# Norm factors through scratch memory instead of through TensorE, and a rebuilt last norm, in a conv + SwiGLU layer on one core

## The chip, the core and the metric

The kernel runs on one core of a Trainium2 chip, as one program. A core has TensorE (PE; its weight loads are shown apart as PEld), VectorE (DVE), ScalarE (ACT), GpSimd (POOL) and SyncE (SP, which here only issues DMAs). ACT issues DMAs too. The metric is the time of one execution in microseconds (us).

## The reference

One layer of a hybrid encoder: 2048 tokens (SEQ) of 1024 features (D_MODEL), all float32. The token mixer is a gated convolution of width 3, followed by a SwiGLU network with 2816 inner features. Every sub-layer is normalized before and after, and the result of a projection of a conditioning vector c gives shift, scale and gate.

```python
def rms_norm(x, g):
    xf = x.astype(jnp.float32)
    y = xf * lax.rsqrt(jnp.mean(xf * xf, axis=-1, keepdims=True) + RMS_EPS)
    return (y * g.astype(jnp.float32)).astype(x.dtype)
...
    h = modulate(rms_norm(x, norm_gains[i, 0]), sh_m, sc_m)
    h = short_conv_mixer(h, conv_w_in[j], conv_w[j], conv_w_out[j])
    x = x + g_m[:, None, :] * rms_norm(h, norm_gains[i, 1])
    h = modulate(rms_norm(x, norm_gains[i, 2]), sh_f, sc_f)
    h = swiglu(h, ffn_w_gate_up[i], ffn_w_down[i])
    x = x + g_f[:, None, :] * rms_norm(h, norm_gains[i, 3])
```

So there are four norms, and each needs one factor per token: one over the root of the mean square of that token's 1024 features.

## The kernel before

**Tiling.** Features lie on the 128 partitions, tokens along the free dimension. The 2048 tokens are handled in two units u of 1024, each of two halves tok of 512 (CH). A tile is 128 features by 512 tokens; a half has eight of them (KD). The four products of the layer are phases: `in` (1024 to 3072), `out` (1024 to 1024), `gu` (1024 to 5632) and `down` (2816 to 1024). The order of the phases is in0, out0, in1, out1, gu0, down0, gu1, down1, where the digit is u.

**A product.** Each product is done with seven half-size products P1 to P7 instead of eight (Strassen's scheme in Winograd's form); sums of blocks of weights and of inputs stand ahead of it. Every operand is split into a high part of fewer bits and the rest (`high`, a cast on ACT; `low`, a subtraction on DVE), and each product of two operands takes three matmuls. Results accumulate in PSUM, whose eight banks are handed out by `bank`.

**The order of the work** is written out by hand. `slots` is the list of (phase, group, product); one slot is twelve matmuls of 128x128 by 128x512 for most of them. The loop at the end of the function goes through the slots; at each it supplies weights some slots ahead, runs what is due, and writes that slot's matmuls. `later(n, f)` runs f n slots on, `schedule` at a slot, and a generator started with `run` sleeps n slots at each `yield n`. Every engine works its instructions in the order in which they are written. SP's queue carries all loads and many stores in one order, so a DMA that must wait holds back those behind it; ACT's queue carries some stores between ACT's own instructions. Buffers come from pools of a fixed number (NRAW = 16 `raw` tiles, NRB = 2 `rb` tiles, and so on), and an instruction that takes a buffer waits until its last reader is done.

**A norm factor.** In the phases `out` and `down`, `add_square` squares each finished tile on ACT and adds the squares up on POOL. `norm_of_sums` multiplies the sum with a column of 1/1024 on PE, which gives four columns of 128 tokens in a bank; DVE adds epsilon. `root` raises to the power -1/2 on POOL and refines the result with a step of Newton's on DVE (three operations on 128x4; the factor comes out times -2, which the gains, multiplied by -0.5 at the start, undo). The factor q then has a token on each partition and must be had along the free dimension, the same on every partition: `diagonal` scales the identity with each of q's four columns on DVE, `spread` multiplies a matrix of ones with the result on PE into a bank and copies it to an `rb` tile on ACT, and `spread_later` puts some slots between the two. The tiles of the half are multiplied with it on DVE. The names in the trace are r0 to r3 for the first norm (from rows of x, four quarters of 512 tokens), n, m (spread as h) and o with u and tok for the other three: n00 is the norm after the mixer of unit 0, half 0. A name's last letter says what it is: v the mean square, p the power, t Newton's step, q the factor, d the diagonal, b the spread in PSUM, r the copy.

r2 and r3 come from `norm_of_rows`, which loads 128 whole rows of x at a time and squares them on ACT with a running sum; r0 and r1 are made in `start`.

**The end.** The last half (u = 1, tok = 1) goes through `last_half`, right behind the last product. The tile before the last adds its square to the other six, the last has its own (`lastq`). `last_half` multiplies the two with the column of 1/1024, adds them, makes root, diagonal and spread (`lasts`, `lastv`, `lastp`, `lastt`, `lastd`, `lastb`), and then for each of eight tiles multiplies z with the factor on DVE. For the five tiles of ON_PE the residual x is added on PE (an identity matmul of x laid down earlier, one of z on top, bank `lastx`), copied by ACT and stored from ACT's queue; for the other three DVE adds it and SP stores it. These tiles are `xl` in the trace.

All instructions are recorded under one line, 78, that of the helper which keeps them in order, so they are told apart by the tiles they write and read.

Of the kernel before, what the change touches and what calls it, by code (L numbers as in the profile page):

```python
# [49 lines left out]
def hybrid_conv_layer(  # L50
# [106 lines left out]
    A.activation(cact, vt[:, VC : VC + KD], AF.Silu)  # L157
    V.tensor_scalar(vt[:, VG : VG + 4 * KD], vt[:, VG : VG + 4 * KD], -0.5, None, ALU.mult)
    mA = [const.tile([P, KD], F32, name=f"mA{i}") for i in range(2)]
# [58 lines left out]
    def root(v, name):  # L218

        p, t = small(4, name + "p"), small(4, name + "t")  # L220
        G.tensor_tensor(p, v, mhalf, ALU.pow)
        yield 1
        q = sb.tile([P, 4], F32, tag="q", bufs=8, name=name + "q")
        V.tensor_tensor(t, p, p, ALU.mult)
        V.tensor_tensor(t, t, v, ALU.mult)
        V.scalar_tensor_tensor(q, t, -3.0, p, ALU.add, ALU.mult)
        return q
# [21 lines left out]
    def spread_later(q, name, put, lag=4):  # L249
        dg = diagonal(q, name)  # L250
        yield lag
        put(spread(dg, name))

    def norm_of_sums(acc, name):

        st = bank(name + "s")
        for t in range(4):
            PE.matmul(st[:, t : t + 1], acc[:, t * P : (t + 1) * P], mean, start=True, stop=True)
        v = small(4, name + "v")
        V.tensor_scalar(v, st[:, :4], EPS, None, ALU.add)  # L260
        yield 1
        return (yield from root(v, name))

    def norm_of_rows(g, name, put):
# [4 lines left out]
        def load(k):  # L269
            if k < len(rows):  # L270
                t, i = rows[k]
                xr[k] = raw(f"xr{g}{t}{i}")
                r0 = g * CH + t * P
                SP.dma_start(xr[k], x[r0 : r0 + P, i * CH : (i + 1) * CH])

# [11 lines left out]
        q = yield from root(v, name)  # L287
        yield 1
        yield from spread_later(q, name, put, 6)

# [223 lines left out]
    class Group:  # L514
# [134 lines left out]
        def ready_z(self, c):  # L649
# [7 lines left out]
            if ph.last and ph.tiles_done[1] == KD:  # L657
                ph.sq = tmp("lastq")
                A.activation(ph.sq[:, :CH], z, AF.Square)
                scaled_z()  # L660
            else:
                add_square(ph.acc, tok, z, f"{ph.name}q{tok}{n}", V if ph.last and c == "21" else G, 0.5 if ph.last else 1)
                if ph.last and tok:
                    later(1, scaled_z)
            ph.tile_ready(tok, n, z)
            if ph.tiles_done[tok] == KD:
                ph.half_ready(tok)

    def add_square(acc, key, z, name, E=G, lag=1):
        if key not in acc:  # L670
            acc[key] = tmp(name)
            A.activation(acc[key][:, :CH], z, AF.Square)
        else:
            sq = tmp(name)
            A.activation(sq[:, :CH], z, AF.Square)
            later(lag, lambda: E.tensor_tensor(acc[key][:, :CH], acc[key][:, :CH], sq[:, :CH], ALU.add))
# [259 lines left out]
    def after_out(ph, tok):  # L936
# [4 lines left out]
        q = yield from norm_of_sums(ph.acc[tok], f"n{u}{tok}")  # L941
        yield (24 if u == 0 else 34) + 8 * tok
        yield from spread_later(q, f"n{u}{tok}", partial(put, rb, 0))
        acc = {}
# [21 lines left out]
        yield 7  # L966
        rb1[u, tok] = yield from norm_of_sums(acc[0], f"m{u}{tok}")

    def after_down(ph, tok):
# [7 lines left out]
        q = yield from norm_of_sums(ph.acc[tok], f"o{u}{tok}")  # L977
        if not ph.last:
            yield 22 + 10 * tok
        yield from spread_later(q, f"o{u}{tok}", partial(put, rb, 0), 2 if ph.last else 4)  # L980
        tiles = {}
# [26 lines left out]

    ON_PE = (4, 5, 6, 7, 0)

    def last_half(ph):
# [7 lines left out]

        st = bank("lasts")  # L1020
        for k in ON_PE[:2]:
            add_x(k)
        for i, sq in enumerate((ph.acc[tok], ph.sq)):
            for t in range(4):
                PE.matmul(col(st, 4 * i + t), sq[:, t * P : (t + 1) * P], mean, start=True, stop=True)
        for k in ON_PE[2:]:
            add_x(k)
        v = small(4, "lastv")
        V.tensor_scalar(v, st[:, :4], EPS, None, ALU.add)
        V.tensor_tensor(v, v, st[:, 4:8], ALU.add)  # L1030
        dg = diagonal(at_once(root(v, "last")), "last")
        b = bank("lastb")
        PE.matmul(b, one, dg[:, :CH], start=True, stop=True)
        for k in ON_PE + tuple(k for k in range(KD) if k not in ON_PE):
            z, xt = ph.z(tok, k), ph.xt[k]
            V.tensor_tensor(z, z, b, ALU.mult)
            if k in ON_PE:
                PE.matmul(sums[k], ident, z, start=False, stop=True, skip_group_check=True)
                A.copy(xt, sums[k])
                A.dma_start(out_tile(u, tok, k), xt)  # L1040
            else:
                V.tensor_tensor(xt, xt, z, ALU.add)
                SP.dma_start(out_tile(u, tok, k), xt)
# [314 lines left out]
    for ph in phases[1:]:  # L1358
# [18 lines left out]
        else:  # L1377
            rb = {}
            src = lambda t, tok, kk, u=ph.u: SP.dma_start(t, x1_d[u][tok][:, kk * 4 : kk * 4 + 4, :])
            for tok, op in ((0, "P1"), (1, "P7")):  # L1380
                go = lambda u=ph.u, tok=tok, rb=rb: run(spread_later(rb1[u, tok], f"h{u}{tok}", partial(put, rb, tok)))
                at(op, -14 - 2 * ph.u, go)
            normalized(Features(ph, src, rb, 1), at, 2 * ph.u)
# [100 lines left out]
```

## Time and profile before

| what | value |
|---|---|
| time, median of 3 runs | 1967.44 us (1966.73 to 1967.90) |
| the profiled execution | 1968.11 us |
| its span in the profile | 1966.3 us |
| PE busy | 1939.7 us, 99% |
| DVE busy | 1463.6 us, 74% |
| ACT busy | 870.3 us, 44% |
| POOL busy | 343.1 us, 17% |
| moved by DMA | 459.51 MB, mean 234 GB/s |
| granted clock of PE | 0.999 |

The span is what the profiler saw of the profiled execution, from its first to its last instruction; 1.8 us lie around it. A row of the timeline gives start and length in us, the engine, the operation, and output <- inputs with their shapes; "x8" merges eight of a kind, and what stands in brackets is how long the engine was idle before and which instruction ended that. ACTq and SPq are the DMA issues of those engines. A row of a wait gives the time in all, how often, and the longest. A row of a tile gives the shortest, median and longest duration in ns.

### The profile page before, as it was taken

The numbers are of one execution on the slowest core, as the hardware profiler recorded it, in microseconds if no ns is written. First come the engines' busy times: TensorE is split into PE (matmuls) and PEld (weight loads), VectorE is DVE, ScalarE is ACT, GpSimd is POOL, SyncE is SP. The second block draws the span as 40 slices with busy tenths as digits, with TensorE's granted clock in tenths as the row PEclk, the third lists the DMA queues.
The fourth block names the chain that finished last, engine by engine and source line by source line (L and its number), as shares of the span: only waits on it lengthen the run. The fifth ranks groups of instructions, "written<-read, shape, count | busy, mean of one in ns | idle before, by whom it ended". The sixth has DMA issues, their size and how long they took to land.

```text
span 1966.3 us, 24998 instructions
## 1 busy us (share of the span) xinstructions
PE 1939.7 (99%) x8468; PEld 1572.9 (80%) x8468; DVE 1463.6 (74%) x2159; ACT 870.3 (44%) x1430; POOL 343.1 (17%) x224
## 2 busy tenths in 40 slices
PE   8899999999999999999999999999999999999998
PEld 4578887878888888888888888888888888888886
DVE  5998898978998876997776765586776655665466
ACT  4633457534336643443333454463333333444452
POOL 0012112311221301244331310120100100111010
PEclk9999999999999999999999999999999999999999
DMA  9369979769996764677665987477554342386534
GB/s 389 137 230 378 332 248 352 267 214 362 324 315 236 263 222 148 223 241 248 208 216 186 304 297 261 183 278 267 199 192 135 125 142 97 118 316 229 197 132 133
DMA packets 204752, 459.51 MB, mean 234 GB/s; under 512 B 22864, under 2 KB 38352, under 8 KB 198224
## 3 DMA queue, kind: packets, MB, share of 16 engines
q1 hardware_dynamic: 180000, 403.52, 59.4%
q10 hardware_dynamic: 24624, 54.40, 7.2%
q8 instruction: 66, 1.08, 0.2%
q14 instruction: 62, 0.51, 0.1%
HBM read 326.75 MB, written 131.07 MB: 233 GB/s over the span
## 4 chain that ended last, share of the span: by engine, by line
PE 92%; DVE 3%; issue 2%; DMA 2%; ACT 1%; POOL 0%; ACTq 0%; POOLq 0%; SPq 0%; DVEq 0%
PE gu0P L78 21%; PE gu1P L78 21%; PE in0P L78 11%; PE down0P L78 11%; PE in1P L78 10%; PE down1P L78 9%; PE out1P L78 4%; PE out0P L78 3%; DMA x<-xx 0%; DMA in0a<-xt_d 0%; DMA c<-c_row_d 0%; PE pms L78 0%; DVE down1z L78 0%; DVE in1y L78 0%; DMA in7P2k<-kin7P 0%
## 5 line engine op out<-in xcount | busy, mean ns | idle before, releaser
L78 DVE TENSOR_TENSOR gu1a<-gu1P,gu1a 128x512 f32<-128x512 f32 x63 | 43.5, 691 | 108.7 <-PE gu1P L78 108.7
L78 DVE TENSOR_TENSOR gu0a<-gu0P,gu0a 128x512 f32<-128x512 f32 x63 | 43.3, 688 | 69.5 <-PE gu0P L78 67.7
L78 POOL TENSOR_TENSOR gu1a<-gu1a 128x512 f32<-128x512 f32 x11 | 19.0, 1726 | 363.5 <-DVE gu1g11s L78 42.5
L78 ACT COPY gu1a<-gu1P 128x512 f32<-128x512 f32 x42 | 24.7, 588 | 98.5 <-PE gu1P L78 87.4
L78 POOL TENSOR_TENSOR nq<-nq,nq 128x512 f32<-128x512 f32 x28 | 41.4, 1477 | 133.8 <-ACT nq L78 129.0
L78 ACT COPY gu0a<-gu0P 128x512 f32<-128x512 f32 x42 | 24.5, 588 | 84.3 <-PE gu0P L78 81.5
L78 DVE CUSTOM_DVE_ANT_0 ada<-ada,c 128x512 f32<-128x512 f32 x80 | 60.1, 761 | 0.0
L78 ACT COPY gu1g<-gu1P 128x512 f32<-128x512 f32 x24 | 14.1, 589 | 92.9 <-PE gu1P L78 92.9
L78 POOL TENSOR_TENSOR down0q<-down0q,down0q 128x512 f32<-128x512 f32 x14 | 23.9, 1706 | 144.1 <-ACT down0q L78 144.0
L78 POOL TENSOR_TENSOR gu0a<-gu0a 128x512 f32<-128x512 f32 x11 | 18.2, 1658 | 170.5 <-ACT gu0a L78 47.5
L78 ACT COPY gu0g<-gu0P 128x512 f32<-128x512 f32 x24 | 14.1, 589 | 75.9 <-PE gu0P L78 75.4
L78 POOL TENSOR_TENSOR down1q<-down1q,down1q 128x512 f32<-128x512 f32 x10 | 16.1, 1615 | 148.6 <-ACT down1q L78 148.5
L78 DVE TENSOR_TENSOR gu1g<-gu1P,gu1g 128x512 f32<-128x512 f32 x24 | 16.6, 691 | 27.4 <-ACT gu1g L78 26.0
L78 DVE TENSOR_TENSOR down2P<-down2P,down2P 128x512 fp32r<-128x512 f32 x14 | 12.0, 854 | 28.6 <-ACT down2P L78 28.6
L78 ACT ACTIVATE gu1a<-gu1a 128x512 f32<-128x512 f32 x42 | 26.6, 633 | 13.2 <-DVE xo L78 6.0
L78 ACT ACTIVATE gu0a<-gu0a 128x512 f32<-128x512 f32 x42 | 26.6, 632 | 11.5 <-DVE gu0a L78 10.2
L78 POOL TENSOR_TENSOR out1q<-out1q,out1q 128x512 f32<-128x512 f32 x14 | 22.3, 1594 | 51.3 <-ACT out1q L78 51.2
L78 POOL TENSOR_TENSOR out0q<-out0q,out0q 128x512 f32<-128x512 f32 x14 | 22.5, 1606 | 45.1 <-ACT out0q L78 44.9
L78 DVE TENSOR_TENSOR xx<-xx,zz 128x512 f32<-128x512 f32 x32 | 28.2, 880 | 1.1
L78 DVE TENSOR_TENSOR gu0g<-gu0P,gu0g 128x512 f32<-128x512 f32 x24 | 16.5, 689 | 14.7 <-ACT gu0g L78 13.3
L78 ACT ACTIVATE nq<-xx 128x512 f32<-128x512 f32 x32 | 20.2, 631 | 15.9 <-DVE xx L78 15.9
L78 DVE TENSOR_TENSOR down10P<-down10P,down10P 128x384 fp32r<-128x384 f32 x14 | 8.6, 615 | 22.0 <-ACT down10P L78 22.0
(3225 smaller groups left out, 6728.5 us busy)
## 6 DMA issues: line engine op xcount, KB each, us to landing
ada<-ada_d SPq DMA_DIRECT2D x64, 256.0 KB, 5.2
act0A<-gu0a SPq DMA_DIRECT2D x33, 256.0 KB, 3.5
act1A<-gu1a SPq DMA_DIRECT2D x33, 256.0 KB, 2.7
ada<-ada_d SPq DMA_DIRECT2D x16, 512.0 KB, 9.4
zz<-z SPq DMA_DIRECT2D x32, 256.0 KB, 5.5
xx<-xt_d SPq DMA_DIRECT2D x32, 256.0 KB, 5.4
x<-xx ACTq DMA_DIRECT2D x32, 256.0 KB, 5.5
down0S<-act0S SPq DMA_DIRECT2D x8, 1024.0 KB, 7.1
```

Of the source, the lines that this page charges most:

```text
L78: return tc.keep_in_program_order(f(*args, **kwargs))
```

## The change

Twelve of the factors (r2, r3, n00 to n11, the four of m, o00 and o01) are no longer spread by diagonal, matmul and copy. `keep_row` stores q, as it is, from ACT's queue to 512 floats of scratch memory, and `repeat_later` loads these 512 floats into all 128 partitions of an `rb` tile through SP's queue. For the factor to come out in token order, q must hold token 4p + t in column t of partition p. So the squares of those norms are written in another order (ACT reads a tile along the tokens and writes with a step of 128 elements), and the rows of x for r2 and r3 are read every fourth.

The step of Newton's goes from `root`, in all places, and the factor of -0.5 on the gains with it.

At the end, the sums of the first seven tiles' squares are multiplied out ahead of the last products (`all_but_one`); the diagonal is multiplied with the ones quarter by quarter; two matmuls into a bank that nobody reads (`lastw`) follow; ON_PE has four tiles; two of the additions go to POOL; the order of the tiles is another one.

```diff
-    V.tensor_scalar(vt[:, VG : VG + 4 * KD], vt[:, VG : VG + 4 * KD], -0.5, None, ALU.mult)
...
     def root(v, name):
 
-        p, t = small(4, name + "p"), small(4, name + "t")
-        G.tensor_tensor(p, v, mhalf, ALU.pow)
+        q = sb.tile([P, 4], F32, tag="q", bufs=8, name=name + "q")
+        G.tensor_tensor(q, v, mhalf, ALU.pow)
         yield 1
-        q = sb.tile([P, 4], F32, tag="q", bufs=8, name=name + "q")
-        V.tensor_tensor(t, p, p, ALU.mult)
-        V.tensor_tensor(t, t, v, ALU.mult)
-        V.scalar_tensor_tensor(q, t, -3.0, p, ALU.add, ALU.mult)
         return q
...
+    def keep_row(q, name, lag=8):
+
+        row = scratch([CH], name + "w")
+        later(lag, lambda: A.dma_start(row.rearrange("(p t) -> p t", t=4), q))
+        return row
+
+    def repeat_later(row, name, put, lag=8):
+        rb = sb.tile([P, CH], F32, tag="rb", bufs=NRB, name=name + "r")
+        SP.dma_start(rb, row.rearrange("(a n) -> a n", a=1).to_broadcast((P, CH)))
+        yield lag
+        put(rb)
...
-                r0 = g * CH + t * P
-                SP.dma_start(xr[k], x[r0 : r0 + P, i * CH : (i + 1) * CH])
+                in_turn = x[g * CH : (g + 1) * CH, i * CH : (i + 1) * CH].rearrange("(p t) c -> p t c", t=4)
+                SP.dma_start(xr[k], in_turn[:, t, :])
...
         q = yield from root(v, name)
-        yield 1
-        yield from spread_later(q, name, put, 6)
+        row = keep_row(q, name, 2)
+        yield 7
+        yield from repeat_later(row, name, put, 6)
...
                 if ph.last and tok:
                     later(1, scaled_z)
+                    if ph.tiles_done[1] == KD - 1:
+                        later(1.5, partial(all_but_one, ph))
...
-    def add_square(acc, key, z, name, E=G, lag=1):
+    def add_square(acc, key, z, name, E=G, lag=1, in_turn=True):
+        def square(t):
+            if in_turn:
+                A.activation(t[:, :CH].rearrange("p (t n) -> p n t", t=4), z.rearrange("p (n t) -> p n t", t=4), AF.Square)
+            else:
+                A.activation(t[:, :CH], z, AF.Square)
...
         q = yield from norm_of_sums(ph.acc[tok], f"n{u}{tok}")
-        yield (24 if u == 0 else 34) + 8 * tok
-        yield from spread_later(q, f"n{u}{tok}", partial(put, rb, 0))
+        row = keep_row(q, f"n{u}{tok}")
+        yield (20 if u == 0 else 30) + 8 * tok
+        yield from repeat_later(row, f"n{u}{tok}", partial(put, rb, 0))
...
-        rb1[u, tok] = yield from norm_of_sums(acc[0], f"m{u}{tok}")
+        q = yield from norm_of_sums(acc[0], f"m{u}{tok}")
+        rb1[u, tok] = keep_row(q, f"m{u}{tok}")
...
-        if not ph.last:
-            yield 22 + 10 * tok
-        yield from spread_later(q, f"o{u}{tok}", partial(put, rb, 0), 2 if ph.last else 4)
+        if ph.last:
+            yield from spread_later(q, f"o{u}{tok}", partial(put, rb, 0), 2)
+        else:
+            row = keep_row(q, f"o{u}{tok}")
+            yield 18 + 10 * tok
+            yield from repeat_later(row, f"o{u}{tok}", partial(put, rb, 0))
...
-    ON_PE = (4, 5, 6, 7, 0)
+    ON_PE, ON_POOL, LAST_TURN = (4, 5, 6, 7), (1, 2), (0, 4, 1, 5, 6, 2, 7, 3)
+
+    def sums_of_squares(ph, sq, first):
+        for t in range(4):
+            PE.matmul(col(ph.st, t + 4 * first), sq[:, t * P : (t + 1) * P], mean, start=True, stop=True)
+
+    def all_but_one(ph):
+        ph.st = bank("lasts")
+        sums_of_squares(ph, ph.acc[1], True)
...
-        st = bank("lasts")
+        v = small(4, "lastv")
+        V.tensor_scalar(v, ph.st[:, 4:8], EPS, None, ALU.add)
         for k in ON_PE[:2]:
             add_x(k)
-        for i, sq in enumerate((ph.acc[tok], ph.sq)):
-            for t in range(4):
-                PE.matmul(col(st, 4 * i + t), sq[:, t * P : (t + 1) * P], mean, start=True, stop=True)
+        sums_of_squares(ph, ph.sq, False)
         for k in ON_PE[2:]:
             add_x(k)
-        v = small(4, "lastv")
-        V.tensor_scalar(v, st[:, :4], EPS, None, ALU.add)
-        V.tensor_tensor(v, v, st[:, 4:8], ALU.add)
-        dg = diagonal(at_once(root(v, "last")), "last")
-        b = bank("lastb")
-        PE.matmul(b, one, dg[:, :CH], start=True, stop=True)
-        for k in ON_PE + tuple(k for k in range(KD) if k not in ON_PE):
+        V.tensor_tensor(v, v, ph.st[:, :4], ALU.add)
+        q = at_once(root(v, "last"))
+        dg = tmp("lastd")
+        b, warm = bank("lastb"), bank("lastw")
+        for t in range(4):
+            c = slice(t * P, (t + 1) * P)
+            V.tensor_scalar(dg[:, c], ident, q[:, t : t + 1], None, ALU.mult)
+            PE.matmul(b[:, c], one, dg[:, c], start=True, stop=True)
+        for _ in range(2):
+            PE.matmul(warm, one, dg[:, :CH], start=True, stop=True)
+        for k in LAST_TURN:
...
-                V.tensor_tensor(xt, xt, z, ALU.add)
+                (G if k in ON_POOL else V).tensor_tensor(xt, xt, z, ALU.add)
...
-                go = lambda u=ph.u, tok=tok, rb=rb: run(spread_later(rb1[u, tok], f"h{u}{tok}", partial(put, rb, tok)))
-                at(op, -14 - 2 * ph.u, go)
+                go = lambda u=ph.u, tok=tok, rb=rb: run(repeat_later(rb1[u, tok], f"h{u}{tok}", partial(put, rb, tok)))
+                at(op, -18 - 2 * ph.u, go)
```

More of the change, by code (lines that the diff above doesn't have):

```diff
@@ L661, in ready_z @@
             else:
-                add_square(ph.acc, tok, z, f"{ph.name}q{tok}{n}", V if ph.last and c == "21" else G, 0.5 if ph.last else 1)
+                add_square(ph.acc, tok, z, f"{ph.name}q{tok}{n}", V if ph.last and c == "21" else G, 0.5 if ph.last else 1, not ph.last)
                 if ph.last and tok:
                     later(1, scaled_z)
+                    if ph.tiles_done[1] == KD - 1:
+                        later(1.5, partial(all_but_one, ph))
             ph.tile_ready(tok, n, z)
@@ L667, in ready_z @@
                 ph.half_ready(tok)
-    def add_square(acc, key, z, name, E=G, lag=1):
+    def add_square(acc, key, z, name, E=G, lag=1, in_turn=True):
[4 more added lines that the diff above has]
+                A.activation(t[:, :CH], z, AF.Square)
         if key not in acc:
             acc[key] = tmp(name)
-            A.activation(acc[key][:, :CH], z, AF.Square)
+            square(acc[key])
         else:
             sq = tmp(name)
-            A.activation(sq[:, :CH], z, AF.Square)
+            square(sq)
             later(lag, lambda: E.tensor_tensor(acc[key][:, :CH], acc[key][:, :CH], sq[:, :CH], ALU.add))
```

## The prediction

> **What bounds the kernel now.** I read the page of the profile first, then PE's own waits, then the chain of waits in order of time.
>
> ```profile
> span 1966.3 us, 24998 instructions
> PE 1939.7 (99%) x8468; PEld 1572.9 (80%) x8468; DVE 1463.6 (74%) x2159; ACT 870.3 (44%) x1430; POOL 343.1 (17%) x224
> ```
> ```profile
> 250.00:300.00 50.00, 50.00 (x220) 41.04 (x219) 46.97 (x102) 25.91 (x54) 3.17 (x2) 1.00 0.78 256
> ```
>
> The second fence has a window: from:to, their length, and busy time of PE, weight loads, DVE, ACT and POOL with counts, granted clock, DMA share, GB/s. PE works for all but 26.6 us of the span. So whatever PE does not have to do anywhere between shortens the run, unless another engine sets the pace at that place. PE's waits (time, count, longest) name such places; those that the change can touch are:
>
> ```profile
> PE in1P L78 <- ACT in1c L78: 2.3, 2, 1.4
> ...
> PE out0P L78 <- ACT out0z L78: 1.7, 1, 1.7
> ...
> PE r1b L78 <- DVE r1d L78: 0.6, 1, 0.6
> ...
> PE in1P L78 <- DMA in7P2k<-kin7P: 0.4, 1, 0.4
> ```
>
> All of these fall before 480 us; from there to the tail PE never idles. The spreads of the norm factors are links of the chain (start, length, what):
>
> ```profile
> 266.19 0.86 PE r2b L78 x2
> ...
> 318.88 0.86 PE r3b L78 x2
> ...
> 361.65 16.32 PE in1P L78 x72
> ...
> 442.19 0.86 PE n00b L78 x2
> ...
> 648.14 0.86 PE h00b L78 x2
> ...
> 1435.14 0.86 PE o01b L78 x2
> ```
>
> From r2b to o01b these are twelve (r2b, r3b, n00b, n01b, n10b, n11b, h00b, h01b, h10b, h11b, o00b, o01b), each 0.86 us of PE. That of the last phase's first half stays.
>
> **The change, part by part.**
>
> *Twelve factors through scratch.* Each loses four DVE scalings of the identity, the 0.86 us on PE and an ACT copy; it gains a store on ACT's queue and a load on SP's. The PE term is 12 x 0.86 = 10.3 us. The lower bound counts only the eight after 600 us, where PE never waits: 6.9 us.
>
> What is moved: each load is issued eight slots before its factor is handed on (six for r2 and r3). A slot is twelve matmuls, 2.72 us (72 in 16.32 us at in1's start), so the lead is 16 to 22 us. The broadcast load of the kernel before, a store of ACT's queue (median us to landing last), and a long wait of SP's queue (in down0) say whether that is enough:
>
> ```profile
> L78 SPq DMA_DIRECT2D c<-c_row_d x8: 327/330/491, 206.7 to 1193.1; - x8
> DMA to landing us min/median/max: 3.7/5.6/8.0
> ...
> x<-xx ACTq DMA_DIRECT2D x32, 256.0 KB, 5.5
> ...
> SPq L78 <- ACT down0z L78: 20.4, 4, 16.3
> ```
>
> The same kind of load landed in 8.0 us at most, so I cost it at nothing. The row's store is issued 12 slots (33 us) before the load, five slots (14 us) for r2 and r3, against the same 8 us; the load therefore finds its row written, and SP, whose queue holds every weight load behind it, should not stop. The two rb buffers are no wait either: n00r serves eight tiles in 19 slots, until 442 + 52 = 494 us, and h00's load comes at 648 - 22 = 626. ACT's queue trades a 0.58 us copy for a 0.34 us issue. r2 and r3 come six slots, 16 us, later: 319 + 16 = 335 us for r3, and in1 begins at 361.65.
>
> *DMA traffic.* Twelve broadcasts add 256 KB each. It matters in one place:
>
> ```profile
> 440.00:450.00 10.00, 10.00 (x44) 7.94 (x43) 5.15 (x9) 3.86 (x8) 0.12 (x1) 1.00 1.03 375
> ...
> 470.00:480.00 10.00, 9.60 (x43) 7.63 (x42) 9.86 (x15) 4.25 (x8) 3.05 (x3) 1.00 1.00 359
> ```
>
> In these windows the DMA engines are full. n01's load, 0.26 MB at 359 GB/s, is 0.7 us, and PE's 1.7 us from n00b and n01b may be waited for again: 0 to 2.4 us lost. I take 0.9, since PE waited only 0.4 us there before.
>
> *Newton's step goes from every root.* Three small DVE operations each. Off the path this is nothing, except at two places. At r1, DVE is the late engine (PE waits 0.6 us for r1d):
>
> ```profile
> 50.87 0.16 DVE L78 TENSOR_TENSOR r1t<-r1p 128x4 f32<-128x4 f32 x1
> ...
> 51.34 0.69 DVE L78 TENSOR_TENSOR in0A12l<-in0b,in0A12h 128x512 fp32r<-128x512 f32 x1
> ```
>
> From 50.87 to 51.34 is 0.47 us; I take 0.4 (0 to 0.47). The second place is r3, where PE's 1.71 us stall at 315.86 begins on DVE:
>
> ```profile
> 308.36 1.25 DVE L78 TENSOR_TENSOR r3t<-r3p 128x4 f32<-128x4 f32 x1
> ...
> 311.13 1.90 DVE L78 TENSOR_SCALAR r3d<-ident,r3q 128x128 f32<-128x128 f32 x4
> ...
> 312.95 0.67 DVE L78 TENSOR_TENSOR out0z<-out0P,out0z 128x512 f32<-128x512 f32 x1
> ...
> 313.66 0.63 ACT L78 ACTIVATE out0q<-out0z 128x512 f32<-128x512 f32 x1 [1.87 <-DVE out0z L78]
> ...
> 315.86 0.73 PE L78 MATMUL out0P<-out0S10h,out0P 128*128 128x512 f32 x2 [1.71 <-ACT out0z L78]
> ```
>
> PE waits for an ACT copy that stands behind a square, and the square waits for a DVE addition held up by r3's Newton step and diagonal: 3.4 us that all go. What is late next is the Silu and the weight cast between, so I take 1.4 of the 1.71 (0 to 1.71).
>
> *Squares written in another order.* ACT reads along the row and writes with a step of 128 elements. No row shows a stepped write on ACT; plain squares take 0.632 us (POOL's sums of them 1.3 to 1.7):
>
> ```profile
> L78 ACT ACTIVATE nq<-xx x32: 617/632/637, 462.5 to 885.5; 128x512 f32<-128x512 f32 x32
> L78 POOL TENSOR_TENSOR nq<-nq,nq x28: 1283/1454/1756, 468.9 to 886.2; 128x512 f32<-128x512 f32 x28
> ...
> 330.00:375.00 45.00, 45.00 (x204) 37.38 (x203) 41.59 (x54) 29.59 (x49) 18.49 (x12) 1.00 0.78 275
> ...
> 394.18 1.91 ACT L78 CAST in1S4h<-in1b 128x2048 fp32r<-128x2048 f32 x1 [5.05 <-DVE in1b L78]
> ```
>
> The cast of 2048 elements takes 1.91 us, so an element costs (1.91 - 0.63)/1536 = 0.83 ns and 0.43 us of a square are streaming. The bounds are no change and a doubled stream, 1.06 us. ACT is 29.6 of 45 us busy where out0's squares lie densest; all 16 of that phase would add 16 x 0.43 = 6.9 us, which fits, so I take zero and keep 6.9 as the far end. [...]
>
> *Rows read every fourth* are the same 2 KB pieces: nothing, covered by a load issued two slots (5.4 us) ahead.
>
> *The end.*
>
> ```profile
> 1941.04 0.68 DVE L78 TENSOR_TENSOR down1q<-down1q,down1q 128x512 f32<-128x512 f32 x1
> ...
> 1941.56 0.62 PE L78 MATMUL down1P<-down1A221h,down7P 128*128 128x512 f32 x2
> ...
> 1948.04 0.95 PE L78 MATMUL lasts<-mean,down1q 128*128 128x1 f32 x8
> ...
> 1948.85 1.03 PE L78 MATMUL lasts<-mean,lastq 128*128 128x1 f32 x8
> ...
> 1949.92 0.16 DVE L78 TENSOR_SCALAR lastv<-lasts 128x4 f32<-128x4 f32 x1 [2.70 <-PE lasts L78]
> ...
> 1951.41 0.16 DVE L78 TENSOR_TENSOR lastt<-lastp 128x4 f32<-128x4 f32 x1 [1.13 <-POOL lastp L78]
> ...
> 1952.00 0.87 DVE L78 TENSOR_SCALAR lastd<-ident,lastq 128x128 f32<-128x128 f32 x4
> ...
> 1954.09 3.68 DVE L78 TENSOR_TENSOR down1z<-down1z,lastb 128x512 f32<-128x512 f32 x6 [1.22 <-PE lastb L78]
> ...
> 1960.45 0.69 DVE L78 TENSOR_TENSOR xl<-xl,down1z 128x512 f32<-128x512 f32 x1
> ...
> DMA  0000000000000000049294999999999972000000
> ```
>
> The sums of seven tiles move ahead of the last products. They free 0.8 us of the tail (1948.04 to 1948.85) and cost PE the same 0.8 plus about 0.2, because the accumulator they read is ready at 1941.72 and PE gets there at 1941.56: -0.2. The early epsilon saves its operation of 0.16, Newton 1952.00 - 1951.41 = 0.6. From the diagonal's start to the first multiplication is 2.09 us; in quarters it is 0.87 for the scalings and one quarter's two passes, which I put at 0.5 (bounds: 0.25, two passes as short as those of the sums, and 1.1, as now), so 0.7 is saved (0.1 to 0.9). Together 1.3 us. The turn behind it has one DVE addition less: 8 x 0.61 + 2 x 0.69 = 6.3 us against 7.05 (1954.09 to 1961.14); two additions go to POOL (1.3 to 1.5 us each, beside the multiplications). r3t's 1.25 us against r1t's 0.16 was a DVE operation beside such a POOL addition, so the last DVE addition, due after 5.6 us, may wait for POOL's second one, 4.4 + 1.4 = 5.8: 0.2 us, inside the bounds. But the stores fill the DMA engines: the last row is their busy share in fortieths of 1950 to 1967 us, and from 1957.2 to 1964.0 eight tiles pass, about 0.8 us each. After, the first tile leaves alone; the second, multiplied after 1.9 us, copied as long after that as now (1956.00 for 1954.77), is issued near 3.8 us, and seven tiles follow one another to about 3.8 + 0.6 + 7 x 0.8 = 10.0 us after the first multiplication; before, 1964.0 - 1954.09 = 9.9. So -0.1, and **1.2 us** for the end (0.3 to 2.2).
>
> The sum is 10.3 + 1.4 + 0.4 + 1.2 - 0.9 = 12.4 us. The profiled execution took 1968.11 us, 0.67 above the median of the runs, 1967.44. 1968.11 - 12.4 = 1955.7, and on the scale of the median **1955.0 us**.
>
> **The rivals.**
>
> *The early spreads buy nothing.* DVE is 94% busy from 250 to 300 us, and DMA full from 440 to 490. Then r2b, r3b, n00b, n01b come back as waits (3.4 us) and r3's stall stays: 6.9 + 0.4 + 1.2 = 8.5 us, 1958.9. Against it: PE is busy for 50.00 of those 50 us, with DVE already that full.
>
> *Slow squares.* If each square of out0 delays the ACT copy for which PE waits, 6.9 us are given back: 1961.9. For it: PE's stall at 315.86 is such a copy. Against: out1, with as many squares, has no PE wait at all. [...]
>
> *More stalls dissolve.* The two waits for in1c (2.3 us) and the one for in7P2k are ACT and SP queues running late; if they go and the traffic costs nothing, 12.4 + 0.9 + 2.7 = 16.0 us, 1951.4.
>
> *Slower: SP stops at the new loads.* If a row's store is late, the load waits at the head of SP's queue and the weights behind it. SP's wait of 16.3 us in down0 passed without PE stopping, so this decides only where a store comes more than some 16 us too late; with 1.4 us of PE idle behind each of the twelve, 16.8 us are lost and it comes out near 1971. Against it: the stores of ACT's queue landed in 5.5 us.
>
> *Nothing changes*: the freed PE time reappears as waits everywhere. Without an idle PE after 480 us there is no sign of it.
>
> **How the numbers follow.** Forecast 0.51, early spreads 0.20, more stalls dissolve 0.14, slow squares 0.08, no change 0.04, slower 0.03. The likeliest gives 1955.0. The range from 1951.2 to 1961.0 takes in the first three cases, 0.85, and leaves the squares' far end out. A difference under 0.2%, 3.9 us, cannot be told from none. All of the first four gain more than that: faster 0.93, same 0.04, slower 0.03.
>
> **What would show it.** PE instructions fall by 24 passes for the twelve spreads; the chain has no r2b to o01b, and PE's gaps after 480 us stay at zero. The 1.71 us wait near 313 us is gone or under 0.5; r1's wait is shorter. The squares' row says 0.63 or 1.06. From the last product's end to the first multiplication before is 7.6 us, after about 5.4. Loads of rows land in under 10 us and SP never waits for a row. It is wrong if PE gains waits on ACT in out0, on DMA between 430 and 500 us, or behind an SP wait for a row.

## The result, and the profile after

The changed kernel takes **1964.32 us** in the median (1960.68 to 1966.38, 17 runs), the kernel before 1967.44 (17 runs beside it): ratio 0.9981, 95% interval 0.9974 to 0.9989. The gain is 3.1 us where 12.4 was forecast. That is under the 6.4 us at the lower end of the predicted range, and under the 3.9 us that the prediction held to be indistinguishable from none, although with 17 runs the interval does exclude no change. The profiled execution took 1963.37 us. Its page begins:

```profile
span 1961.6 us, 24893 instructions
PE 1934.4 (99%) x8450; PEld 1569.8 (80%) x8450; DVE 1446.7 (74%) x2061; ACT 898.0 (46%) x1417; POOL 344.9 (18%) x226
```

PE is busy 5.3 us less than before, where the twelve spreads alone were to take off 10.3, so half of that is missing from PE's own work too; the span is 4.7 us shorter. PE's waits of after (time, count, longest):

```profile
PE r0b L78 <- DVE r0d L78: 3.8, 1, 3.8
PE in1P L78 <- ACT in1c L78: 3.4, 2, 2.6
...
PE out0P L78 <- ACT out0z L78: 1.7, 1, 1.7
...
PE gu0P L78 <- ACT gu0a L78: 0.6, 1, 0.6
...
PE in1P L78 <- ACT in1b L78: 0.4, 1, 0.4
...
PE in1P L78 <- ACT in1C L78: 0.3, 1, 0.3
```

The wait for r0d was 0.2 us before; by 127 us nothing of it is left. The wait for in1c has grown from 1.4 to 2.6 us, the one for out0z is as long as before but at another place, and those for gu0a (711 us), in1b and in1C stand behind 480 us, where there were none. Laying PE's instructions of the two traces side by side shows where the change gains and loses. This is the ledger (us, negative is gained; it adds up to the span's difference within 0.4):

| place in the trace of before | after against before |
|---|---|
| head, to 127 us | 0.0 |
| the twelve spreads, together | -10.6 |
| 301.6 | +0.7 |
| the stall at 315.86 / a new one at 321 | -1.9 / +1.8 |
| 433.7, the wait for in1c | +1.1 |
| 435 to 437 | +1.6 |
| 484, 541, 549, 563 | +1.5 |
| 711, the wait for gu0a | +0.8 |
| 895 | +0.2 |
| the end | -0.3 |

The largest loss is the one at 433 to 437 us. The chain of waits of after, from 425 us (start, length, what), and PE's timeline behind it show it:

```profile
425.68 6.79 DMA kgu0P<-gu0P
...
433.06 0.59 ACT in1c L78
```
```profile
433.69 0.73 PE L78 MATMUL in1P<-in1S1h,in0P 128*128 128x512 f32 x2 [2.60 <-ACT in1c L78]
...
435.40 1.06 PE L78 MATMUL in1P<-in1S1h,in0P 128*128 128x512 f32 x2
```
```profile
434.70:438.20 3.50, 3.50 (x10) 2.76 (x9) 1.07 (x2) 0.00 (x0) 3.46 (x2) 0.53 0.90 314
```

The store of kgu0P, 512 KB, lands 6.8 us after its issue. ACT's queue stands still until then, because the buffer that is being stored is to be written again, and the copy in1c, for which PE waits, stands behind it in that queue. The last fence is a window (length, busy of PE, weight loads, DVE, ACT, POOL, granted clock, DMA share, GB/s): behind the wait the clock is granted at 0.53, so PE is "busy" and does 10 matmuls, where the kernel before does 17 in the same 3.50 us at a clock of 1.00. The trace's clock record has it at a half for 3.413 us, from 434.9 us on, which costs 1.7 us. I call this a half-speed window. The record of after has two more ahead of the tail, from 15.1 and 73.1 us, and that of before one, from 83.9 us, each 3.413 us long. One execution of each kernel was profiled, and the granted clock of the 17 runs of the change goes from 0.995 to 0.998, so by my estimate the number of such windows (one takes off 0.0009, half of 3.413 us in 1962) is not the same in each.

Squares with a stepped write, and the end:

```profile
L78 ACT ACTIVATE nq<-xx x32: 1114/1162/1177, 462.8 to 884.5; 128x512 f32<-128x512 f32 x32
```
```profile
1937.39 1.05 PE L78 MATMUL lasts<-mean,down1q 128*128 128x1 f32 x8
...
1943.19 1.88 PE L78 MATMUL lastx<-xl,ident 128*128 128x512 f32 x4
...
1948.77 0.69 DVE L78 TENSOR_TENSOR down1z<-down1z,lastb 128x512 f32<-128x512 f32 x1 [0.66 <-PE lastb L78]
```
```profile
DMA  0000000000000078000099999999999961000000
```

The square went from 0.632 to 1.162 us. The last row is the DMA engines' busy share in fortieths of 1945 to 1962 us: the first tile leaves alone, then comes a hole, then all others at full share. The rows' loads land in under 10 us, as forecast; the slowest:

```profile
L78 SPq DMA_DIRECT2D h01r<-m01w x1: 320/320/320, 639.6 to 639.6; - x1
...
DMA to landing us min/median/max: 8.7/8.7/8.7
```

But SP's queue did stop for DMAs of rows (time, count, longest, between 300 and 330 us):

```profile
SPq L78 <- DMA r3w<-r3q: 4.9, 1, 4.9
...
SPq L78 <- DMA r3r<-r3w: 1.5, 1, 1.5
```

Two more such stops follow, 0.9 us for n01r and 0.8 for h00r, 8.1 us in all. In none does a row's load wait for its store. In the traces the DMAs of SP and ACT signal their landing on eight semaphores, shared out evenly (1421 DMAs before, 177 or 178 on each; 1445 after, 180 or 181), and in all landings recorded no DMA is issued before the last one on its semaphore has landed: SP stopped ahead of a load of `ada` which uses semaphore 108, as r3's store does; that store lands at 319.08 us and the load is issued at 319.14. In both traces there are at most eight DMAs under way, and each row's store and load takes one of these eight places.

### The profile page after: what moved, and what is told of

The parts are those of the page before. It is cut to its first block, busy times and chain, and to the rows that moved or that the text cites. A ratio compares the mean times of both kernels' runs of the same rounds, so it can differ in the third digit from the quotient of the medians.

```text
span 1961.6 us, 24893 instructions
## 1 busy us (share of the span) xinstructions
PE 1934.4 (99%) x8450; PEld 1569.8 (80%) x8450; DVE 1446.7 (74%) x2061; ACT 898.0 (46%) x1417; POOL 344.9 (18%) x226
## 3 DMA queue, kind: packets, MB, share of 16 engines
q8 instruction: 66, 1.08, 0.2%
## 4 chain that ended last, share of the span: by engine, by line
PE 81%; DVE 9%; DMA 5%; ACT 3%; issue 2%; SPq 0%; ACTq 0%; POOL 0%; DVEq 0%
PE gu1P L78 21%; PE gu0P L78 20%; PE down0P L78 11%; PE down1P L78 11%; PE in0P L78 9%; PE in1P L78 4%; PE out1P L78 2%; PE out0P L78 1%; DMA x<-xx 1%; PE pms L78 1%; DMA kgu0P<-gu0P 0%; DVE in1b L78 0%; DMA xr<-x_d 0%; DMA out2P<-w_out_d 0%; DVE in1y L78 0%
## 5 line engine op out<-in xcount | busy, mean ns | idle before, releaser
L78 ACT ACTIVATE nq<-xx 128x512 f32<-128x512 f32 x32 | 37.1, 1159 | 15.7 <-DVE xx L78 15.7
L78 ACT ACTIVATE down0q<-down0z 128x512 f32<-128x512 f32 x16 | 18.5, 1153 | 14.9 <-DVE down0z L78 14.8
```

The costliest lines, as they stand in the source:

```text
L78: return tc.keep_in_program_order(f(*args, **kwargs))
```

## The experiments

Ratios are to the kernel before, run on the same chip beside each; half their intervals is about 0.0009, 1.7 us, so a difference between two of them carries about 2.5 us. "Of after" means an edit of the changed kernel. The diffs are cut at `...`.

**e1_plain_squares**, of after: the squares as before; the order is made where the sums are read.

```diff
-            PE.matmul(st[:, t : t + 1], acc[:, t * P : (t + 1) * P], mean, start=True, stop=True)
+            part = acc[:, :CH].rearrange("p (n t) -> p t n", t=4)[:, t, :] if in_turn else acc[:, t * P : (t + 1) * P]
+            PE.matmul(st[:, t : t + 1], part, mean, start=True, stop=True)
```

> The changed kernel with the squares written in plain order again; the order that the stored factors need comes from the weight loads of the sums, which read every fourth column of the accumulator. The results stay the same. Theory S (the stepped squares, 1.15 us for 0.63, hold up ACT and with it PE in in1, out1 and gu0): the squares fall back to 0.63 us, PE's waits at 541, 564 and 711 us go (2.5 us with what they drag along), and the time is 2 to 3 us under the changed kernel's, about 1961.5. Theory P (the time won early is paid back by loads and DVE chains whatever the squares cost): no change, 1964.3 within 1 us.

Measured: 1967.45, ratio 0.9998 (0.9989 to 1.0007), slower than the change, which neither theory had. The stepped read has a price of its own. The weight loads of one sum, in this run and in after (shortest/median/longest, ns):

```profile
L78 PEld LDWEIGHTS m01s<-mean,nq x8: 308/329/332, 559.6 to 561.2; 128*128 128x128 f32 x8
```
```profile
L78 PEld LDWEIGHTS m01s<-mean,nq x8: 187/192/192, 560.4 to 561.3; 128*128 128x128 f32 x8
```

Each of the ten sums holds PE 1.89 us for 1.04, 8.5 us in all, yet the run lost only 3.1 against the change. The ledger says where part of the rest went: +3.2 us against after at 377 us had become -0.9 by 479. Half of this is one half-speed window of 1.7 us for another: this run has one at 321.7 us and none at 434.9. The rest is 1.7 us of two longer sums, which came back by 400 us; PE's wait of 0.85 us for in1c at 395 us of after is gone, for one. So PE work added there came out nearly even, as PE work removed did. The stall at 321 us stands in this run too (1.8 us), so the stepped squares didn't make it; the one at 711 is gone. The run can't price the squares; e4 does.

**e4_stepped_squares**, of before: only the squares' write is stepped (so the factors fall on other tokens than they should).

```diff
+        def square(t):
+            if in_turn:
+                A.activation(t[:, :CH].rearrange("p (t n) -> p n t", t=4), z.rearrange("p (n t) -> p n t", t=4), AF.Square)
...
-            A.activation(sq[:, :CH], z, AF.Square)
+            square(sq)
```

> The kernel before with nothing but the squares of all norms but the last phase's written with a step of 128 elements; spreads, Newton's step and end as before. The factors then fall on other tokens of the same half; the work is the same. Theory S: ACT's squares take 1.15 us and the time rises by 1 to 3 us to about 1969.5. Theory P: ACT has room, 1967.4 within 0.7 us.

Measured: 1968.57, ratio 1.0001 (0.9992 to 1.0010). A square nearly twice as long costs the kernel before nothing that can be measured.

**e2_spreads_on_pe**, of after: spreads, squares and rows as before; the power alone and the new end stay. **e3_old_end**, of after, with the end of before. **e8_power_only**, of before, without Newton's step and its scaling.

```diff
-        row = keep_row(q, f"n{u}{tok}")
-        yield (20 if u == 0 else 30) + 8 * tok
-        yield from repeat_later(row, f"n{u}{tok}", partial(put, rb, 0))
+        yield (24 if u == 0 else 34) + 8 * tok
+        yield from spread_later(q, f"n{u}{tok}", partial(put, rb, 0))
```

> The changed kernel with the twelve factors spread by diagonal, matmul and copy as before, squares and rows in plain order: what is left of the change is the root without Newton's step and the rebuilt end. If the end and Newton's step are worth what the prediction gave them (1.2 + 1.8 us): 1964.4. If they are worth next to nothing (0.2 us at the end, r3's stall only moved): 1967, and the change's gain of 3.1 us lies in the spreads alone.

> The changed kernel with the end of the kernel before (its root without Newton's step). If the rebuilt end is worth 1.2 us without Newton's 0.6: 1965.0. If the profile's ledger is right (0.2 us in all): 1964.3 to 1964.5, the changed kernel's own time.

> The kernel before with the Newton step alone taken out (with the scaling of vt that served it); nothing else is changed, so this parts the 2.3 to 2.7 us that the run with spreads on TensorE gained into Newton and new end. If Newton's leaving is the gain (the old end in the whole change was no slower, 1963.6): 1965.2, with the stall at 315.86 down from 1.7 to 0.5 us and the wait at 433 at 1.1. If the new end is: 1967.4.

Measured: e2 1965.2, 0.9984 (0.9976 to 0.9993); e3 1963.64, 0.9979 (0.9970 to 0.9988); e8 1965.11, 0.9990 (0.9981 to 0.9998). Newton's leaving is worth about 2 us alone. What the new end is worth is not shown: without it the change is no slower (e3), while e2, which has it, is 0.0006 or 1.2 us ahead of e8, which has not, and both differences lie within 2.5 us of none. All twelve spreads together, beside the power and the end, change the ratio from 0.9984 to 0.9981 only.

**e6_code_shift**, of after: short products in the head, where PE waits for r0d anyway. **e11_before_shifted**, of before: three warm-up products for eight. Both are meant only to move PE's instructions, and with them the loading of PE's code, against the work. The diff is e6's:

```diff
         warm(8)
+        for _ in range(9):
+            PE.matmul(b[:, :16], one, w[:, :16], start=True, stop=True)
```

> The whole change, with nine short products (16 columns, 18 passes, 36 instructions of TensorE) behind the warm-up of the head, where TensorE waits 3.8 us anyway. Theory F (TensorE's code is loaded in blocks of 16 KB, 256 instructions, one block holding one of the 16 DMA engines for 0.93 to 1.25 us; with fewer instructions ahead a block came into the middle of the store of kgu0P at 425.7 us, 3.2 us behind its issue where it had been 0.3 us, and made the wait at in1c 1.2 us longer and the half-speed window behind it): the block comes about 4 us sooner against the work, the store lands 5.4 us after its issue and not 6.8, the wait at 433 falls from 2.6 to about 1.4 us, the window of 434.8 to 438.2 is gone: 1964.3 - 1.2 - 1.6 = 1961.5. Rival R (the rows' own traffic or their DMA issues delay that store): nothing changes there, 1964.3.

> The kernel before with three warm-up products in the head for eight, so that TensorE's code runs 20 instructions later against the work and nothing else changes. Theory F (the position of the code blocks against the store of kgu0P): the block at 427.1 us comes some 2 us behind the store's issue, as in the change, the store lands 6.6 to 6.8 us after its issue for 5.5, the wait at 433 rises from 1.4 to 2.3 to 2.6 us, perhaps with a half-speed window behind it: 1968.5, with the window 1970. If the blocks don't matter: 1967.4 and 1.4 us.

Measured: e6 1961.57, 0.9972 (0.9961 to 0.9982). The median is what theory F said, but against the change the gain is 2.75 us by the medians, 1.8 by the ratios, whose intervals overlap, and 1.4 between the two profiled executions. PE at the same place in e6:

```profile
432.56 0.73 PE L78 MATMUL in1P<-in1S1h,in0P 128*128 128x512 f32 x2 [0.78 <-ACT in1c L78]
```

The wait is 0.8 us for 2.6, and no half-speed window follows it. But in e6 one stands at 321.6 us, behind a wait of 1.8 us, where after had none behind 1.7; this is why the profiled executions differ by half of the forecast only. The busy share of the DMA engines from the issue of that store to its landing, in fortieths, in after (425.7 to 432.5 us) and in e6 (426.4 to 431.4), with the queue that brings code:

```profile
DMA  9999711339999999999998510101000000000959
...
q8 instruction: 1, 0.02, 0.9%
```
```profile
DMA  9999945421635999896999989998886610000000
```

In after the transfer is nearly through at slice 23, 429.6 us, and then single packets trickle (24 GB/s, one packet of 4 KB in each slice of 0.17 us) until near 432. The code block came at 428.99 us and took 0.98, to 429.97; from 429.95 to 432.00 ten packets of 4 KB follow one another end to end. The trace has 16 signals of the store's landing: fifteen by 430.30 us, the last at 432.46, 2.2 us behind (in before by 431.68 and at 432.44, 0.8 behind). In e6 the block had come before the store, and there is hardly such a tail. All profiled kernels at this store:

```
                     block behind the     issue to the cast
                     store's issue, us    that waits for it, us
before, e2, e4, e5, e8, e10, e13, e14
                     -0.1 to 0.5          5.4 to 5.7
e7, e12              0.5, 0.0             5.6, 6.0
e1, after, e3        1.9, 3.3, 3.4        6.6, 6.9, 6.7
e9, e6               -2.2, -2.5           5.3, 5.0
e11                  3.9                  4.8
```

So with a block 1.9 to 3.4 us behind the issue the store is 0.9 to 1.2 us later than in the kernel before; far ahead of it or behind the transfer's bulk the store is sooner. Kernels that load the early rows stand in three of these lines (e7 and e12; e1, after and e3; e6), so it is not the rows that part them. e11 came out at 1969.33 (1.0010, 1.0001 to 1.0018), near the forecast, but not for its reason: the block overshot the store (3.9 us behind the issue, where about 2 was meant), PE's wait there fell to 0.6 us, and the time was lost in the head, 2.3 us by 90 us, where PE had two half-speed windows (13.9 to 20.8 us) behind the shorter warm-up. So only e6 tested the blocks as forecast. In the trace of before there are 66 such blocks (`q8 instruction: 66, 1.08` on its page), 16 KB each, on 17,030 instructions of PE, one per 258, where theory F has 256; that they are PE's code follows from their moving with PE's instructions, 5.8 us sooner against the store with 36 more ahead (e6) and 3.6 later with 20 fewer (e11).

**e7_rows_unused**, of e2: every row is stored and loaded where the change does it, into the buffer that the copy of the product then overwrites. **e12_rows_narrow**: the same with each load to one partition. **e14_places_only**: the same without stores and loads. **e13_stores_only**: e2 with the stores alone. The diff shows e7's way of taking a factor, against the changed kernel:

```diff
         rb = sb.tile([P, CH], F32, tag="rb", bufs=NRB, name=name + "r")
         SP.dma_start(rb, row.rearrange("(a n) -> a n", a=1).to_broadcast((P, CH)))
-        yield lag
-        put(rb)
+        yield lag - 4
+        dg = diagonal(q, name)
+        yield 4
+        put(spread(dg, name, rb))
```

> The run with all spreads on TensorE, Newton step gone and the new end (1965.2), and beside it every row stored and loaded at the same places as in the change, into the same buffer, which the copy of TensorE's product then overwrites: the traffic and the issues of the rows without their saving. Theory R (the rows' stores and loads cost time in the stretches bound by DMA): the waits of the change come back at 433 (2.6 us) and between 479 and 563 (+1.2), with a half-speed window or two: 1967.5 to 1969. Theory F (it is where the code blocks fall, and TensorE's instructions are as many as before): 1965.2, the wait at 433 at 1.1 us.

> The run with all spreads on TensorE and every row stored and loaded unused (1970.1), but each row's load goes to one partition, 2 KB and not 256 KB; the stores, every issue and its place stay, and the copy of TensorE's product overwrites what is loaded. Theory D (the 12 x 256 KB that the loads move are what costs): the waits go, back to the run without rows, 1965.2. Rival I (the issues on SP and ACT, and the stores in 16-byte pieces): 1970.1. Of the 4.9 us between, what remains is the issues' and stores' share.

> The run with all spreads on TensorE (1965.2), and beside it each factor's store to scratch, 12 issues on ACT with 128 pieces of 16 bytes each; no row is loaded, and every spread stands where it stood. Theory S16 (the stores are what the rows cost, through their pieces or the 12 issues of 0.33 us on ACT): 1968 to 1969. Rival Z (the later place of r2 and r3, or the loads' issues): 1965.2.

> The run with every row stored and loaded unused (1970.1; with narrow loads 1969.3), without the stores and without the loads: what stays of it is the place of r2's and r3's products, six slots later, and that the factors' buffers are taken when the loads would be issued. Theory Z (the place): 1968 to 1969. Rivals S16 and the loads' issues: 1965.2. What is left between this run, the stores alone and 1969.3 is the issues of the loads on SP.

Measured, as a ladder: e2 0.9984, e14 0.9985 (1965.35 us; 0.9976 to 0.9994), e13 0.9994 (1967.09; 0.9986 to 1.0003), e12 1.0006 (1969.29; 0.9997 to 1.0015), e7 1.0014 (1970.13; 1.0005 to 1.0023). The places cost nothing that can be measured. Stores and loads together cost 0.0030, 5.9 us, give or take 2.5: some 2 us for the stores, 2.4 for the issues of the loads, 1.6 for their 3 MB. Each of these three steps is no larger than its uncertainty, so the sum is shown and its parts are not: e13 lies between its two theories, e12 near rival I. e7 is above what theory R said, but PE's wait at 433 stayed at 1.3 us, as theory F had it. PE's instructions are as many in e7 as in e2 (17,044 and 17,043), and the code block falls on the store alike. The windows show the cost as idle PE, in e2 and in e7 (columns as above):

```profile
300.00:345.00 45.00, 44.22 (x191) 35.34 (x190) 39.41 (x57) 35.86 (x60) 12.89 (x8) 1.00 0.93 343
430.00:490.00 60.00, 58.87 (x256) 47.95 (x256) 49.01 (x81) 23.69 (x42) 10.59 (x7) 1.00 1.00 355
500.00:700.00 200.00, 200.00 (x892) 164.60 (x891) 185.09 (x282) 106.28 (x181) 45.28 (x30) 1.00 0.81 283
```
```profile
300.00:345.00 45.00, 42.70 (x182) 34.13 (x183) 37.23 (x56) 33.93 (x56) 14.97 (x8) 1.00 0.92 337
430.00:490.00 60.00, 57.42 (x247) 45.86 (x246) 48.70 (x80) 23.09 (x41) 9.54 (x7) 1.00 0.96 336
500.00:700.00 200.00, 198.88 (x888) 163.88 (x887) 184.30 (x280) 103.95 (x179) 46.68 (x31) 1.00 0.82 287
```

In these windows PE is idle 1.9 us in e2 and 6.0 in e7; the change has 6.1 (it is busy for 42.59, 56.93 and 199.39 us). By the ledger of e7 against e2, 3.9 of 4.7 us are lost by 617 us, so it is mostly the early rows that cost. Between 500 and 700 us PE is busy for the whole 200.00 in every kernel without early rows (before, e2, e4, e5, e8, e9, e10, e14) and for 198.66 to 199.68 in every one with them, e13's mere stores included.

**e5_late_rows**, of after: rows only for n10, n11, h10, h11, o00, o01; the other six factors through PE. **e9_longer_warm_up** and **e10_sums_later** are e5 with `warm(12)` for `warm(8)`, and with `later(2.5, ...)` for `later(1.5, ...)` ahead of `all_but_one`.

```diff
-        row = keep_row(q, f"n{u}{tok}")
-        yield (20 if u == 0 else 30) + 8 * tok
-        yield from repeat_later(row, f"n{u}{tok}", partial(put, rb, 0))
+        if u == 0:
+            yield 24 + 8 * tok
+            yield from spread_later(q, f"n{u}{tok}", partial(put, rb, 0))
+        else:
+            row = keep_row(q, f"n{u}{tok}")
...
```

> The change with its rows kept only for the later norms (n10, n11, h10, h11, o00, o01); the factors r2, r3, n00, n01, h00, h01 go through TensorE as before, with plain squares. Theory E (the early rows' savings are paid back before 712 us, the late ones are kept): the gain of the run with all spreads on TensorE (1965.2) stays, and six passes of 0.87 us come off: 1965.2 - 5.2 = 1960.0, with no PE wait over 1.2 us at in1c near 433. Rival K (rows bring a cost wherever they are): the late ones bring no more than the early ones did, 1963.5 to 1964.5.

> The run with the late rows alone (1960.8) and, in the head, twelve warm-up products for eight. That run's trace has two half-speed windows from 13.7 to 20.5 us, behind a wait of TensorE of 2.8 us for r0d, and stands 1.9 us later than the kernel before at 87 us. Theory H (the warm-up, no longer queued behind the scaling of vt, ends 4 us too soon and lets the clock fall): the wait and the windows are gone, the head is back at about 0, 1959.0. Rival B (what the head loses is taken up by 127 us, where the work waits for a load and VectorE): 1960.8.

> The run with the late rows alone (1960.8), with the sums of the seven tiles one slot (2.8 us) further back among the last products. If what they cost TensorE there beyond their own time is the wait for the accumulator (0.48 us in the change's trace): +1.1 us at 1938 becomes +0.7, 1960.4. If they cost TensorE 1.1 us wherever they stand, or push the last sums back: 1960.8 or more.

Measured: e5 **1960.82**, 0.9963 (0.9951 to 0.9976); e9 1961.86, 0.9974 (0.9963 to 0.9985); e10 **1960.64**, 0.9962 (0.9949 to 0.9974). Half of the spreads left on PE is 3.5 us faster than none (0.0018, give or take 0.0014), near theory E. What the six late rows save is kept: e5's lead over the kernel before grows by 5.2 us from 480 to 1437 us (1.7 to 6.9), and SP's queue never stops for a row in it. e9 came out as neither theory said. It met the head's half of its forecast (no wait for r0d, no window there) and lost it elsewhere: at 423.11 us the code block coincided with an issue on SP's queue that took 1.97 us for some 0.4, the store behind it was issued 1.2 us late, and a half-speed window followed from 431.5. e10 is level with e5, and their times cannot part its two theories; in its trace the sums cost 0.9 us of the stream for e5's 1.2, which is the first theory's direction.

e5 and e10 have the same instructions on PE up to the sums at 1935 us, and still e10 loses 2.0 us at 890. There ACT's cast of gu10P stands behind a store that is issued 0.08 us (e5) and 0.07 us (e10) after a load of gu12b, on the same semaphore, has landed. First e5, then e10:

```profile
888.94 0.62 ACT L78 CAST gu10P<-gu10b 128x512 fp32r<-128x512 f32 x1 [1.80 <-DMA gu12b<-w_gu_d]
```
```profile
890.94 0.62 ACT L78 CAST gu10P<-gu10b 128x512 fp32r<-128x512 f32 x1 [3.87 <-DMA gu12b<-w_gu_d]
```

In e5 the code block came at 888.80, when the load had landed (888.49); in e10 it came at 888.43, and the load landed at 890.50. That the block delayed the load is argued from the times alone.

## Why the prediction was wrong

**The spreads** were sized rightly, 10.3 against 10.6 us; all 24 passes are gone. That a saved pass shortens the run held behind 712 us, as the argument from PE's missing idle time had it.

**The step that failed is the price of the way through scratch**: "so I cost it at nothing" for the loads, no term for the stores and the issues, and 0.9 us (0 to 2.4) for the traffic. It measured 5.9 us, give or take 2.5 (e7 against e2), most of it ahead of 620 us. I asked of each row only whether it would arrive in time. It did (8.7 us at most). What I didn't ask is what the rows delay: in the windows above the DMA engines are 0.81 to 1.00 busy, PE waits there for copies by ACT that stand behind stores, and the early six factors bring twelve more DMAs into just that stretch. That the loss comes by this way is argued. A likely part of it is the eight semaphores, which the prediction left out where it said that SP's queue "should not stop": it stopped four times for rows' DMAs in the change (8.1 us) and never in e5, and from 240 to 700 us an issue follows within 0.12 us of the landing that freed its semaphore 77 to 91 times in the kernels that load the early rows (78 in after; e1, e3, e6, e7) and 62 to 74 times in the others (71 in before; e12 records too few landings to tell). But e13, with the stores alone, has 67, and no run shows what such a stop costs PE. How the 2 us of the stores come about stays open too: the trace of after has 9 ns in the median for each of the 1536 pieces of 16 bytes, and 0.33 us of ACT's queue for an issue; no run parts the pieces from the issue.

**A second cost had no term**: PE's code blocks. Fewer instructions ahead moved one into a store, for 1.1 us of waiting and 1.6 of half speed in the profiled execution. e6 shows the wait gone with the block, without touching the rest; its 1.4 to 2.75 us are the likely size of this cost, not a firm one.

**r3's stall** was to leave 1.4 us and did leave 1.9, but 1.8 stood at 321 us again:

```profile
318.75 1.90 ACT L78 CAST out0S40h<-out0S 128x2048 fp32r<-128x2048 f32 x1 [3.63 <-DMA out0S<-y0S]
```
```profile
321.18 0.73 PE L78 MATMUL out0P<-out0S10h,out2P 128*128 128x512 f32 x2 [1.69 <-ACT out0z L78]
```

ACT's cast of out0S waits for a load that lands 8 us after its issue, in before (312.0 to 319.9) as in after, and the copy out0z, for which PE waits, comes behind that cast. Before, PE's stall at 315.86 and r3b's 0.9 us filled this time; without them PE got there sooner and waited. In e2, e5 and e8, which keep r3b there, the stall at 315.86 is down to 0.5 to 0.6 us and none follows at 321.

**Newton** was 0.4 + 1.4; e8 has 2.0 us. r1's 0.46 was there at 53 us and gone by 127.

**The squares**: the row took the far bound and a little more, 1.16 us for 1.06. Nothing in the trace of before had shown what a stepped write costs, and that the far bound was the right one is luck. Zero for the kernel was right for the kernel before (e4); in the change 0.8 us at 711 went with it (e1).

**The end**: from the last product to the first multiplication 5.4 us, as forecast. But the sums took 1.2 us out of the stream for the 0.8 they left free, and from the first multiplication to the end of the span it is 12.8 us for 12.2; the second tile leaves 2.5 us after the first (six fortieths in the row above). The net is 0.3 for 1.2 in this trace.

By these terms: 10.6 + 2.0 + 0.3 - 5.9 - 2.7 - 0.8 = 3.5 us against 3.1 measured. They carry some 3 us of uncertainty and come from different runs, so that they close is in part luck and no proof of each.

Of the rivals, **early spreads buy nothing** was the right kind at the wrong size: taking them from PE costs. **SP stops at the new loads** did not occur as described, a load waiting for its row's store, but SP did stop for rows' DMAs in the way shown above. PE's wait on ACT in out0 and SP's waits for rows are signs that the prediction had named as making it wrong; the wait around 433 us is on ACT, with a store ahead of it.

## What to carry to other kernels

In this kernel a PE instruction removed was worth its time only where nothing else set the pace. Where PE already had waits on copies behind DMAs, work added or removed came out nearly even, and moving it to more DMAs was a loss. So make such an exchange stage by stage, and begin where the windows show PE busy for all of their length and the DMA engines not full. After a change of instruction count, look where the code blocks and the half-speed windows have moved before believing a difference of 2 us.

## What the hardware showed that was not expected

- A block of TensorE's code (16 KB) took 1.33 us (before) and 0.98 us (after) of a DMA engine at the store of kgu0P, 0.88 to 2.08 in the whole of before, and with one 1.9 to 3.4 us behind its issue that store was 0.9 to 1.2 us later; nine short products in an idle head moved it away.
- A weight load that reads every fourth float takes 0.33 us (e1) for 0.19 (after), and an ACT square that writes with a step of 512 bytes 1.16 (after) for 0.63 (before).
- The clock fell to a half for 3.413 us behind single waits of PE of 1.8 and 2.0 us (e6 and e3, at 322 us) and of 2.6 us (after, at 434), not behind one of 1.7 (before and after, out0z). The length of the wait alone doesn't decide it: e1's 2.4 us at 435 had no window behind it, and of the 1.8 us that PE waits at 71 to 74 us in all kernels a window follows in thirteen and none in before, e7 and e9.
